# Later turning of the feed-forward products, and more seven-product steps in the down projection

## The chip, the cores and the metric

The kernel runs on one core of one Trainium2 chip. The metric is the device time of one execution in microseconds (us); several executions are summed up by their median. Before the change three runs have a median of 1989.0 us (1987.55 to 1989.62).

## What is computed

An encoder trunk of two layers on 256 tokens of width 2048, all in float32: attention and a feed-forward block, then a gated recurrence and a feed-forward block. The change is in the feed-forward blocks alone:

```python
def swiglu(h, w_gate, w_up, w_down):
    return (jax.nn.silu(h @ w_gate) * (h @ w_up)) @ w_down
...
        x = x + mix
        x = x + swiglu(rms_norm(x, norm_ffn[i]), ffn_w_gate[i], ffn_w_up[i], ffn_w_down[i])
```

The hidden width D_FF is 5632, which is 44 tiles of 128.

## The kernel before

**Products.** Every float32 operand is held as a sum of two parts, `hi` and `lo`, that TensorE takes at full speed, and a product of two blocks is three matmuls (high by high, high by low, low by high; `product`, L342 to L347). The tokens, 128 at a time, are the stationary operand; 512 weight columns stream past them. A weight tile of 128 rows by 1024 elements ("half", `load_half`) comes by DMA on SP's queue (SyncE) into `raw` (5 buffers); ScalarE (ACT) casts it to `hi` (L132) and VectorE (DVE) subtracts to get `lo` (L133), 5 buffers each.

**Pairs.** `project_pair` makes two column blocks (j = 0, 1) for both halves of the tokens (a = 0, 1) at once, in four PSUM accumulators (tag `acc`, 4 buffers in all). A step is two tiles of 128 along the contraction. A plain step is 2 halves and 8 products, 24 matmuls. A seven-product step is Strassen's scheme in Winograd's form on the 2 by 2 blocks (tokens by columns): `seven_forms` makes block sums of the weights, `x_forms` block sums of the left operand, and 7 products, 21 matmuls, do for 8. Such a step loads one half to `raw` as usual, the first half of the next one to `wx` (SP, 256 KB), and that next one whole to `sr` (GpSimd's DMA queue, POOL), whose second part is added onto its first part by an accumulating DMA (L293, L294; 2 buffers, fetched ahead by `fetch_next`). DVE then makes the sums (L307, L311, L312) and three low parts (L313, L315, L316), ACT three casts (L309, L310, L314). `wx`, `wxh` and `wxl` have one buffer each. After the last seven-product step of a pair, `merge` (L380) adds four product sums (tag `pm`) into `fg` and `fu`.

**Feed-forward.** The 44 hidden tiles go in parts of 12, 16 and 16 (PARTS). A part first runs one unit for every 4 hidden tiles: gate and up as a pair of 8 steps, seven-product in steps 2, 4 and 6 (THREE, counted from 0 as 1, 3, 5; the very first unit of a layer has two). At its end `done` applies Silu and the product (L842 to L846), and then the result `fu` is turned so that hidden rows lie on partitions: one block transpose on DVE (L515, `tb`), 16 copies of 32 by 256 on ACT (L523, `tf`), then the split into high and low part (L857 ACT, L858 DVE, `act`). After its 3 or 4 units a part multiplies by its rows of w_down: `down`, two pairs (columns 0 and 1, then 2 and 3). Of the sixteen-tile parts the pairs have 8 steps, seven-product in steps 3 and 6 (TWO); of the twelve-tile part 6 steps, all plain, and the last two steps are taken one column after the other. The second pair of the last part in the first layer has plain steps only, since it feeds the next norm. `done` in `down` adds accumulators to the residual (L575), `middle` the merged sums (L567).

**Order.** TensorE's (PE's) order is that of the program text. The other engines' orders are set by a scheduler at build time, from the text, with the chain of casts (`in_line`) held in order. Each engine runs its list strictly in order.

Of the kernel before, what the change touches and what calls it, by code (L numbers as in the profile page):

```python
# [12 lines left out]
F32 = mybir.dt.float32  # L13
F32R = mybir.dt.float32r
AF = mybir.ActivationFunctionType
ALU = mybir.AluOpType
AX = mybir.AxisListType

P = 128
# [54 lines left out]
def trunk(ctx, tc, w, out):  # L74
# [86 lines left out]
    def down_seven(n, alone):  # L161
        return () if alone or n == SHORT else TWO
# [169 lines left out]

    def project_pair(xs, forms, plan, middle, done):
# [19 lines left out]
        for n, cols in plan:  # L353
            if n in forms:
                s1, s2, s3, s4 = forms[n]
                b11, b21, t3, b22, t1, t2, t4 = seven_forms()
                if n == seven[0]:
                    p1, q6, q5, q7 = (ps_m.tile([P, WIDE], F32, tag="pm", name=nm("pm")) for _ in range(4))
                last = n == seven[-1]
                product(p1, tokens(2 * n, 0), b11, last)  # L360
                product(bank(0, 0), tokens(2 * n + 1, 0), b21)
                product(bank(1, 0), s4, b22)
                product(q7, s3, t3, last)
                product(q5, s1, t1, last)
                product(q6, s2, t2, last)
                product(bank(0, 1), tokens(2 * n + 1, 1), t4)
                if last:
                    middle(p1, q5, q6, q7)
                continue
            end = n == plan[-1][0]  # L370
            for j in cols:
                half()
                hi, lo = (flat(t) for t in newest["tiles"])
                for a in range(2):
                    for k in range(2):
                        product(bank(j, a), tokens(2 * n + k, a), (hi[:, k, :], lo[:, k, :]), end and k == 1)
                if end:
                    done(j, banks[j])
# [132 lines left out]
    def turned(src, both=True, behind=None, whole=False):  # L511
        b = fp[0].tile([P, 2, FOUR, P], F32, tag="tb", name=nm("tb"))
        f = fp[0].tile([P, 8, FOUR, 32], F32, tag="tf", name=nm("tf"))
        if whole:
            dve.transpose(b, src)  # L515
        for a in () if whole else range(2):
            dve.transpose(b[:, a, :, :], src[:, a, :])
# [8 lines left out]
        return f[:].rearrange("p q k t -> p k q t") if whole else [f[:, :, k, :] for k in range(FOUR)]  # L526
# [33 lines left out]
    def down(xs, forms, norm=None, end=False):  # L560
        for c in (0, 2):
# [7 lines left out]
            def done(j, accs):  # L569
                for a in range(2):  # L570
                    n = 2 if end and c + j == NCOL - 1 else 1
                    for i in range(n):
                        sl = slice(i * WIDE // n, (i + 1) * WIDE // n)
# [8 lines left out]
            project_pair(xs, {} if alone else forms, down_plan(len(xs) // 2, alone), middle, done)  # L582
# [247 lines left out]
    def ffn(norm, nxt):  # L830
# [4 lines left out]
        def unit(hid, forms, parts, i):  # L835
# [16 lines left out]
            u = got[1]  # L852
            first = len(hid)
            f = turned(u, False, whole=True)
            h = act_tiles()
            hi, lo = (h[:, :, o : o + S].rearrange("p k (q t) -> p k q t", t=32) for o in (0, S))
            act.copy(hi, f)  # L857
            dve.tensor_tensor(lo, f, hi.bitcast(F32), ALU.subtract)  # L858
            hid.extend(h[:, k, :] for k in range(FOUR))
            for k, n in enumerate(TWO):  # L860
                if parts == KT and first <= 2 * n < len(hid):
                    forms[n] = x_forms(hid[2 * n], hid[2 * n + 1], f"hf{k}")

        line.update(act=None, dve=None)
        for p, n in enumerate(PARTS):
            hid, forms = [], {}
            for i in range(n // FOUR):
                unit(hid, forms, n, sum(PARTS[:p]) // FOUR + i)
# [3 lines left out]
            down(hid, forms, nxt if last else None, last and nxt is None)  # L872
# [221 lines left out]
```

## Time and profile before

| | |
|---|---|
| median of three runs | 1989.0 us |
| profiled execution: its own time | 1986.64 us |
| profiled execution: span, first to last instruction | 1984.7 us |
| DVE busy | 1690.3 us (85%) |
| ACT busy | 1346.5 us (68%) |
| POOL busy | 279.5 us (14%) |
| granted TensorE clock, mean | 1.000 |
| DMA moved, mean rate | 426.98 MB, 215 GB/s |

Busy time is the time in which an engine has at least one instruction under way. On DVE and ACT the spans of neighbours overlap a little, so the distance between two starts in a busy stretch is shorter than the mean duration. Matmuls overlap more, and their pace is read from starts or counts.

### The profile page before, as it was taken

The page shows a single profiled execution, that of the slowest core. Times are in us where ns is not written, and L with a number is a line of the kernel's source. Part 1 is how long each engine was busy: PE and PEld are TensorE (multiplying, and loading weights), DVE is VectorE, ACT ScalarE, POOL GpSimd, SP SyncE. Part 2 cuts the span into 40 slices and gives each one's busy share as a digit, 9 for nine tenths or more (in the row PEclk, how much of TensorE's full clock was granted, in tenths as well). Part 3 has the DMA queues.
Part 4 walks back from the last instruction along what each step waited for, and adds up shares of the span by engine and source line. Part 5 has one row for each costly group of instructions (what it writes and reads, how often), then busy time and mean ns, then how long its engine had stood idle before and what let it go on. Part 6 is the DMA issues. An engine that isn't in the chain of part 4 may idle for free.

```text
span 1984.7 us, 28163 instructions
## 1 busy us (share of the span) xinstructions
PE 1969.9 (99%) x9890; PEld 1676.1 (84%) x9890; DVE 1690.3 (85%) x2355; ACT 1346.5 (68%) x2085; POOL 279.5 (14%) x369
## 2 busy tenths in 40 slices
PE   9999999999999999999999999999999999999999
PEld 8898888888887888888899998888888887888877
DVE  8998788857898888989878977898768998889986
ACT  7666666655777556777799987767646676567763
POOL 2563001000010010001034331001001010011000
PEclk9999999999999999999999999999999999999999
DMA  8444767767677777666655657566757777677773
GB/s 321 158 144 139 226 186 241 241 204 233 212 232 221 249 248 236 205 227 221 207 175 183 191 160 228 190 214 219 249 191 226 230 249 249 204 242 236 232 255 131
DMA packets 131469, 426.98 MB, mean 215 GB/s; under 512 B 14720, under 2 KB 15488, under 8 KB 131200
## 3 DMA queue, kind: packets, MB, share of 16 engines
q1 hardware_dynamic: 108720, 363.81, 53.5%
q0 software_dynamic: 22464, 61.35, 13.1%
q8 instruction: 78, 1.28, 0.3%
q14 instruction: 63, 0.52, 0.1%
q10 hardware_dynamic: 144, 0.02, 0.0%
HBM read 423.03 MB, written 2.10 MB: 214 GB/s over the span
## 4 chain that ended last, share of the span: by engine, by line
PE 72%; DVE 14%; issue 6%; ACT 5%; DMA 2%; POOL 0%; SPq 0%; DVEq 0%; ACTq 0%; POOLq 0%
PE acc L344 40%; PE acc L273 9%; PE pm L344 6%; DVE lo L133 5%; PE acc L251 4%; ACT tf L523 4%; PE acc L391 3%; PE acc L390 3%; PE acc L392 3%; DMA raw<-in_w_gate_dram 1%; PE pm L392 1%; PE pm L391 1%; PE pm L390 1%; DVE lo L313 1%; ACT wxh L314 1%
## 5 line engine op out<-in xcount | busy, mean ns | idle before, releaser
L133 DVE TENSOR_TENSOR lo<-raw,hi 128x1024 fp32r<-128x1024 f32 (+1 forms) x630 | 762.3, 1227 | 164.1 <-ACT hi L132 154.9
L132 ACT CAST hi<-raw 128x1024 fp32r<-128x1024 f32 (+1 forms) x630 | 647.8, 1044 | 346.4 <-PE acc L344 198.5
L344 PE MATMUL acc<-hi,xg 128*128 128x512 f32 x1920 | 613.7, 389 | 1.7 <-DVE fg L842 1.6
L344 PEld LDWEIGHTS acc<-hi,xg 128*128 128x128 f32 x1920 | 360.3, 188 | 77.9 <-DVE fg L842 2.5
L344 PE MATMUL acc<-hi,act 128*128 128x512 f32 x1212 | 378.8, 389 | 0.2 <-DVE fu L845 0.2
L344 PE MATMUL acc<-lo,xg 128*128 128x512 f32 x960 | 373.5, 389 | 0.0
L344 PEld LDWEIGHTS acc<-hi,act 128*128 128x128 f32 x1212 | 227.5, 188 | 47.9 <-issue 0.6
L344 PE MATMUL acc<-lo,act 128*128 128x512 f32 x606 | 235.8, 389 | 0.0
L344 PEld LDWEIGHTS acc<-lo,xg 128*128 128x128 f32 x960 | 180.2, 188 | 37.4
L523 ACT COPY tf<-tb 32x256 f32<-32x256 f32 x448 | 180.7, 403 | 30.7 <-DVE tb L515 24.8
L273 PE MATMUL acc<-hi,act 128*128 128x512 f32 x512 | 160.0, 390 | 0.0
L293 POOL DMA_DIRECT2D sr<-in_w_up_dram x64 | 35.5, 555 | 842.3 <-DVE lo L313 807.7
L391 PE MATMUL acc<-xg,hi 128*128 128x256 f32 x512 | 144.8, 283 | 0.6 <-DVE xg L468 0.6
L390 PE MATMUL acc<-xg,hi 128*128 128x256 f32 x512 | 144.9, 283 | 0.1
L392 PE MATMUL acc<-xg,lo 128*128 128x256 f32 x512 | 144.4, 282 | 0.0
L344 PEld LDWEIGHTS acc<-lo,act 128*128 128x128 f32 x606 | 113.7, 188 | 23.7
L251 PE MATMUL acc<-xg,hi 128*128 128x512 f32 x384 | 126.0, 397 | 0.1
L316 DVE TENSOR_TENSOR wxl<-raw,wxh 128x1024 fp32r<-128x1024 f32 x78 | 95.2, 1220 | 28.6 <-ACT wxh L314 28.6
L314 ACT CAST wxh<-raw 128x1024 fp32r<-128x1024 f32 x78 | 82.0, 1051 | 47.4 <-DVE raw L312 46.5
L273 PEld LDWEIGHTS acc<-hi,act 128*128 128x128 f32 x512 | 96.1, 188 | 19.6
L309 ACT CAST hi<-sr 128x1024 fp32r<-128x1024 f32 x78 | 82.0, 1051 | 44.6 <-PE acc L344 39.4
L273 PE MATMUL acc<-lo,act 128*128 128x512 f32 x256 | 99.6, 389 | 0.0
(246 smaller groups left out, 3289.2 us busy)
## 6 DMA issues: line engine op xcount, KB each, us to landing
raw<-in_w_gate_dram SPq DMA_DIRECT2D x176, 512.0 KB, 5.3
raw<-in_w_down_dram SPq DMA_DIRECT2D x162, 512.0 KB, 4.9
raw<-in_w_up_dram SPq DMA_DIRECT2D x112, 512.0 KB, 5.6
sr<-in_w_up_dram POOLq DMA_DIRECT2D x64, 512.0 KB, 4.7
raw<-in_w_in_dram SPq DMA_DIRECT2D x64, 512.0 KB, 4.4
raw<-in_w_qv_dram SPq DMA_DIRECT2D x40, 512.0 KB, 4.2
raw<-in_w_o_dram SPq DMA_DIRECT2D x32, 512.0 KB, 3.6
wx<-in_w_up_dram SPq DMA_DIRECT2D x64, 256.0 KB, 4.5
```

The lines of the kernel that those rows point to most:

```text
L132: newest["cast"] = in_line("act", act.copy(hi[:, sl, :], raw[:, sl, :]))
L133: in_line("dve", dve.tensor_tensor(lo[:, sl, :], raw[:, sl, :], hi[:, sl, :].bitcast(F32), ALU.subtract))
L251: pe.matmul(o, w, x, start=(k == 0 and not part), stop=(k == total - 1 and not part))
L273: pe.matmul(accs[a], x, wt[:, k, :], start=(k0 + k == 0 and n == 0), stop=(end and k == 1 and n == 2))
L309: in_line("act", act.copy(hi, raw))
L314: in_line("act", act.copy(xh[:, 1:, :], r1))
L316: in_line("dve", dve.tensor_tensor(xl[:, 1:, :], r1, xh[:, 1:, :].bitcast(F32), ALU.subtract))
L344: pe.matmul(acc, a, b, start=id(acc) not in begun, stop=last and i == 2)
L390: pe.matmul(o, hi, x[:, :S], start=start, stop=False)
L391: pe.matmul(o, hi, x[:, S:], start=False, stop=False)
L392: pe.matmul(o, lo, x[:, :S], start=False, stop=stop)
L523: n = turn(o, y)
```

## The change

Three things change. `down_seven` gives the sixteen-tile down pairs seven-product steps 2, 4 and 6 (before: 3 and 6) and the twelve-tile pairs steps 2 and 4 (before: none). `x_forms` is accordingly called for the hidden tiles of the first, second and third unit of a sixteen-tile part and of the first two units of a twelve-tile part. And the turning of a unit's result no longer stands in the text at the unit's end: it is cut into six pieces (transpose, four groups of four copies, split and block sums) that `settle` runs inside the next `project_pair`: three at each seven-product step, one at each half of a plain step that isn't the first, all that are left before a step that takes one column. The copies are held behind the newest cast on ACT. The matrices `tb` and `tf` have the same size as before.

```diff
     def down_seven(n, alone):
-        return () if alone or n == SHORT else TWO
+        return () if alone else THREE[:2] if n == SHORT else THREE
...
+    owed = []
+
+    def settle(n=1):
+        while owed and n:
+            owed.pop(0)()
+            n -= 1
...
-        for n, cols in plan:
+        for i, (n, cols) in enumerate(plan):
             if n in forms:
                 s1, s2, s3, s4 = forms[n]
                 b11, b21, t3, b22, t1, t2, t4 = seven_forms()
+                settle(3)
...
+            if len(cols) == 1:
+                settle(-1)
             end = n == plan[-1][0]
             for j in cols:
                 half()
+                if i:
+                    settle()
...
-            u = got[1]
-            first = len(hid)
-            f = turned(u, False, whole=True)
-            h = act_tiles()
-            hi, lo = (h[:, :, o : o + S].rearrange("p k (q t) -> p k q t", t=32) for o in (0, S))
-            act.copy(hi, f)
-            dve.tensor_tensor(lo, f, hi.bitcast(F32), ALU.subtract)
-            hid.extend(h[:, k, :] for k in range(FOUR))
-            for k, n in enumerate(TWO):
-                if parts == KT and first <= 2 * n < len(hid):
-                    forms[n] = x_forms(hid[2 * n], hid[2 * n + 1], f"hf{k}")
+            def transposes():
+                kept["b"], kept["f"] = (fp[0].tile([P, 2 * FOUR, P], F32, tag=n, name=nm(n), bufs=1) for n in ("tb", "tf"))
+                dve.transpose(kept["b"], got[1])
+
+            def copies(q):
...
+                for i in range(4):
+                    n = act.copy(f[32 * i : 32 * i + 32, q::4, :, :], b[32 * q : 32 * q + 32, :, i, :, :])
+                    follow(n, line["act"])
+
+            def split_tiles():
...
+                act.copy(hi, f)
+                dve.tensor_tensor(lo, f, hi.bitcast(F32), ALU.subtract)
+                hid.extend(h[:, k, :] for k in range(FOUR))
+                for k, n in enumerate(THREE):
+                    if n in down_seven(parts // 2, False) and first <= 2 * n < len(hid):
+                        forms[n] = x_forms(hid[2 * n], hid[2 * n + 1], f"hf{k}")
+
+            owed.extend([transposes, *(partial(copies, q) for q in range(4)), split_tiles])
```

In the orders below a name stands for a buffer's use (`act_2701` is one unit's split hidden tiles), and line numbers of the changed kernel are larger by some lines: L842/L852 and L845/L855 take accumulators into `fg` and `fu`, L846/L856 make the hidden product, L515/L869 transpose, L523/L875 copy, L857/L882 and L858/L883 split, L575/L585 release accumulators, L383 to L386 / L395 to L398 merge, L567/L577 add the merged sums.

**First place: DVE where the first twelve-tile down pair of the second layer begins.** Before:

```order
L845 TENSOR_TENSOR fu_2686_14230<-acc_2641_14011,fu_2686_14230 128x512
L846 SCALAR_TENSOR_TENSOR fu_2686_14230<-fu_2686_14230,nr_2483_13212,fg_2685_14229 128x512 x2
L133 TENSOR_TENSOR lo_2720_14416<-raw_2718_14414,hi_2719_14415 128x1024
L515 STREAM_TRANSPOSE tb_2699_14316<-fu_2686_14230 128x1024
L133 TENSOR_TENSOR lo_2723_14434<-raw_2721_14432,hi_2722_14433 128x1024
L133 TENSOR_TENSOR lo_2726_14452<-raw_2724_14450,hi_2725_14451 128x1024
L133 TENSOR_TENSOR lo_2729_14470<-raw_2727_14468,hi_2728_14469 128x1024
L858 TENSOR_TENSOR act_2701_14335<-tf_2700_14317,act_2701_14335 128x4x256
```

Now, the same stretch up to the transpose and the next load:

```order
L855 TENSOR_TENSOR fu_2731_14383<-acc_2681_14132,fu_2731_14383 128x512
L856 SCALAR_TENSOR_TENSOR fu_2731_14383<-fu_2731_14383,nr_2524_13345,fg_2730_14382 128x512
L312 TENSOR_TENSOR raw_2754_14509<-raw_2754_14509 128x512
L313 TENSOR_TENSOR lo_2761_14521<-sr_2711_14264,hi_2760_14520 128x1024
L315 TENSOR_TENSOR wxl_2759_14517<-wx_2757_14515,wxh_2758_14516 128x512
L856 SCALAR_TENSOR_TENSOR fu_2731_14383<-fu_2731_14383,nr_2524_13345,fg_2730_14382 128x512
L316 TENSOR_TENSOR wxl_2759_14517<-raw_2754_14509,wxh_2758_14516 128x1024
L133 TENSOR_TENSOR lo_2771_14571<-raw_2769_14569,hi_2770_14570 128x1024
L869 STREAM_TRANSPOSE tb_2763_14533<-fu_2731_14383 128x1024
L133 TENSOR_TENSOR lo_2774_14593<-raw_2772_14591,hi_2773_14592 128x1024
```

and a little later, up to the low half of the split:

```order
L313 TENSOR_TENSOR lo_2782_14625<-sr_2729_14358,hi_2781_14624 128x1024
L315 TENSOR_TENSOR wxl_2780_14621<-wx_2778_14619,wxh_2779_14620 128x512
L316 TENSOR_TENSOR wxl_2780_14621<-raw_2775_14613,wxh_2779_14620 128x1024
L133 TENSOR_TENSOR lo_2789_14674<-raw_2787_14672,hi_2788_14673 128x1024
L133 TENSOR_TENSOR lo_2792_14692<-raw_2790_14690,hi_2791_14691 128x1024
L883 TENSOR_TENSOR act_2784_14637<-tf_2764_14534,act_2784_14637 128x4x256
```

The transpose now stands behind the whole set of block sums of step 2, and the low half of the split behind those of step 4 and two more loads, where only plain loads stood.

**Second place: ACT where a sixteen-tile down pair of the second layer begins.** Before:

```order
L309 CAST hi_3088_16333<-sr_3033_16032 128x1024
L310 CAST wxh_3086_16329<-wx_3085_16328 128x512
L523 COPY tf_3064_16225<-tb_3063_16224 32x2x128 x16
L314 CAST wxh_3086_16329<-raw_3082_16322 128x1024
L132 CAST hi_3096_16372<-raw_3095_16371 128x1024
L132 CAST hi_3099_16390<-raw_3098_16389 128x1024
L132 CAST hi_3102_16408<-raw_3101_16407 128x1024
L132 CAST hi_3105_16426<-raw_3104_16425 128x1024
L857 CAST act_3065_16243<-tf_3064_16225 128x4x256
L132 CAST hi_3108_16444<-raw_3107_16443 128x1024
```

Now:

```order
L309 CAST hi_3150_16504<-sr_3101_16248 128x1024
L310 CAST wxh_3148_16500<-wx_3147_16499 128x512
L603 ACTIVATE fg_3120_16366<-fg_3120_16366,nr_2524_13345 128x512
L314 CAST wxh_3148_16500<-raw_3144_16493 128x1024
L132 CAST hi_3160_16554<-raw_3159_16553 128x1024
L132 CAST hi_3163_16576<-raw_3162_16575 128x1024
L132 CAST hi_3166_16598<-raw_3165_16597 128x1024
L309 CAST hi_3171_16608<-sr_3119_16342 128x1024
L875 COPY tf_3154_16518<-tb_3153_16517 32x2x128 x16
L310 CAST wxh_3169_16604<-wx_3168_16603 128x512
L314 CAST wxh_3169_16604<-raw_3165_16597 128x1024
```

The sixteen copies still stand together on ACT. Before, they stood between the first (L310) and the second (L314) cast of the block sums of the pair's first seven-product step, step 3; now they stand ahead of both of these casts of the second one, step 4, and step 2 has its casts ahead of them.

**Third place: DVE at the end of the first column of that twelve-tile pair.** The two accumulators of column 0 are `acc_2705` and `acc_2706` before, `acc_2747` and `acc_2748` now; the second pair takes over the four buffers in the order in which the first took them. Before:

```order
L133 TENSOR_TENSOR lo_2749_14584<-raw_2747_14582,hi_2748_14583 128x1024
L575 TENSOR_TENSOR x_tok_75<-x_tok_75,acc_2705_14344 128x512
L575 TENSOR_TENSOR x_tok_75<-x_tok_75,acc_2706_14351 128x512
L133 TENSOR_TENSOR lo_2754_14604<-raw_2752_14602,hi_2753_14603 128x1024
L133 TENSOR_TENSOR lo_2757_14622<-raw_2755_14620,hi_2756_14621 128x1024
```

Now:

```order
L585 TENSOR_TENSOR x_tok_75<-x_tok_75,acc_2747_14475 128x512
L397 TENSOR_TENSOR fg_2785_14661<-pm_2768_14547,fg_2785_14661 128x512
L398 TENSOR_TENSOR fu_2786_14662<-fu_2786_14662,pm_2768_14547 128x512
L577 TENSOR_TENSOR x_tok_75<-x_tok_75,fu_2786_14662 128x512
L133 TENSOR_TENSOR lo_2811_14790<-raw_2809_14788,hi_2810_14789 128x1024
L307 TENSOR_TENSOR wx_2812_14794<-wx_2812_14794,raw_2809_14788 128x512
L577 TENSOR_TENSOR x_tok_75<-x_tok_75,fg_2785_14661 128x512
L577 TENSOR_TENSOR x_tok_75<-x_tok_75,fu_2786_14662 128x512
L585 TENSOR_TENSOR x_tok_75<-x_tok_75,acc_2752_14495 128x512
L311 TENSOR_TENSOR raw_2809_14788<-sr_2762_14530,raw_2809_14788 128x512
L585 TENSOR_TENSOR x_tok_75<-x_tok_75,acc_2748_14482 128x512
```

Two neighbours have come apart: nine instructions now stand between the release of column 0's first accumulator and that of its second. The end of the first pair of the last part in the first layer looks alike.

34 lines of the change are left out of this document (20 added, 14 removed).

## The prediction

> **What bounds the kernel now.** I read the page's head, then windows over the stages of the second layer's feed-forward, then TensorE's waits, then the timelines of the places where it waits. First the head, an undisturbed window, and four stages: the first twelve-tile down pair, the first and the third unit of a sixteen-tile part, and that part's first down pair. The columns are the stretch, its length, then PE, PE's weight loads, DVE, ACT and POOL (busy time and instructions), the granted clock, DMA share and rate.
>
> ```profile
> span 1984.7 us, 28163 instructions
> PE 1969.9 (99%) x9890; PEld 1676.1 (84%) x9890; DVE 1690.3 (85%) x2355; ACT 1346.5 (68%) x2085; POOL 279.5 (14%) x369
> 1430.00:1590.00 160.00, 160.00 (x707) 132.48 (x707) 127.35 (x144) 94.97 (x120) 11.86 (x17) 1.00 0.70 222
> 1410.80:1443.50 32.70, 32.70 (x146) 27.09 (x145) 21.56 (x22) 19.88 (x30) 0.00 (x0) 1.00 0.66 212
> 1517.60:1559.10 41.50, 41.50 (x185) 34.37 (x184) 36.93 (x43) 29.08 (x42) 4.23 (x6) 1.00 0.76 241
> 1600.70:1642.30 41.60, 41.60 (x184) 34.10 (x183) 39.36 (x50) 30.05 (x43) 4.24 (x6) 1.00 0.75 231
> 1642.30:1685.50 43.20, 41.81 (x183) 34.06 (x182) 37.07 (x43) 27.89 (x39) 2.82 (x4) 1.00 0.71 233
> ```
>
> TensorE sets the time: 706 intervals in 160 us are 0.2266 us per matmul, and 160 us pass without a gap, at a clock of 1.00. So a matmul that goes away in a feed-forward stage takes 0.2266 us with it, as long as the engines that feed it keep up. DVE comes next: it has 2.2 us to spare in the third unit (41.60 less 39.36), 11 us in the twelve-tile pair. Now the only waits of any weight in those stages, and one of the four places in detail, TensorE's starts first, then ACT, then DVE:
>
> ```profile
> PE pm L344 <- DVE wxl L316: 3.0, 4, 0.8
> PE pm L344 <- ACT wxh L314: 2.3, 4, 0.7
> ...
> 1656.33 0.39 PE L344 MATMUL pm<-wxh,hf 128*128 128x512 f32 x1
> 1657.35 0.50 PE L344 MATMUL pm<-wxh,hf 128*128 128x512 f32 x1 [0.63 <-ACT wxh L314]
> 1658.61 0.50 PE L344 MATMUL pm<-wxl,hf 128*128 128x512 f32 x1 [0.76 <-DVE wxl L316]
> 1658.95 0.40 PE L344 MATMUL pm<-wxh,hf 128*128 128x512 f32 x1
> ...
> 1646.51 0.62 ACT L310 CAST wxh<-wx 128x512 fp32r<-128x512 f32 x1 [0.21 <-DVE wx L307]
> 1649.59 6.63 ACT L523 COPY tf<-tb 32x256 f32<-32x256 f32 x16 [2.46 <-DVE tb L515]
> 1656.25 1.04 ACT L314 CAST wxh<-raw 128x1024 fp32r<-128x1024 f32 x1
> 1657.20 3.89 ACT L132 CAST hi<-raw 128x1024 fp32r<-128x1024 f32 x4
> ...
> 1648.32 1.24 DVE L515 STREAM_TRANSPOSE tb<-fu 128x1024 f32<-128x1024 f32 x1
> 1657.33 1.23 DVE L316 TENSOR_TENSOR wxl<-raw,wxh 128x1024 fp32r<-128x1024 f32 x1 [5.46 <-ACT wxh L314]
> ```
>
> The reader is to see a queue: the 16 copies that turn the last unit's result take ACT 6.63 us, the cast L314 stands behind them, DVE's L316 behind that, and TensorE behind both. Three intervals (1656.33 to 1658.95) take 2.62 us instead of 0.68: 1.94 us lost, where the waits view counts 1.39 (0.63 and 0.76). There are four such places, one at the start of each sixteen-tile down. Scaled from 1.39 to 1.94, their 5.3 us in the waits view (3.0 and 2.3) are 7.4 us.
>
> **The change part by part.**
>
> *Fewer matmuls.* A seven-product step has 21 matmuls for 24. The first layer gains two in each of two twelve-tile pairs and one in each of three sixteen-tile pairs (the fourth stays plain), the second layer two in two and one in four: 7 and 8. 15 steps by 3 matmuls by 0.2266 us are 10.2 us less.
>
> The Trainium skill, "TensorE: Matmul & The Clock Gate", section "Wait — 56ns, not 53.3ns?", gives 215.7 ns between starts for 512 columns on a warm array; the trace has 226.6 here, and the measurement decides. By the page it would be an estimated 9.7 us.
>
> *More work on DVE, ACT and DMA.* Their prices come from the page's groups and a busy stretch of DVE:
>
> ```profile
> L133 DVE TENSOR_TENSOR lo<-raw,hi 128x1024 fp32r<-128x1024 f32 (+1 forms) x630 | 762.3, 1227 | 164.1 <-ACT hi L132 154.9
> L316 DVE TENSOR_TENSOR wxl<-raw,wxh 128x1024 fp32r<-128x1024 f32 x78 | 95.2, 1220 | 28.6 <-ACT wxh L314 28.6
> ...
> 1601.57 0.68 DVE L311 TENSOR_TENSOR raw<-sr,raw 128x512 f32<-128x512 f32 x1
> 1602.17 0.68 DVE L845 TENSOR_TENSOR fu<-acc,fu 128x512 f32<-128x512 f32 x1
> 1606.43 1.22 DVE L316 TENSOR_TENSOR wxl<-raw,wxh 128x1024 fp32r<-128x1024 f32 x1
> 1607.57 1.22 DVE L133 TENSOR_TENSOR lo<-raw,hi 128x1024 fp32r<-128x1024 f32 x1
> ```
>
> From start to start a 128x512 operation takes 0.60 us and a 128x1024 one 1.14. A plain step costs DVE two L133, 2.28 us; a seven-product step three of 1.14 (L133, L313, L316) and four of 0.60 (L307, L311, L312, L315), 5.82: 3.54 more, 53 us over 15 steps. TensorE needs 24 x 0.2266 = 5.44 us for a plain step and 4.76 for the other. The block sums of the hidden tiles are made 16 times, not 8; the third unit, which has one set, shows 2.4 us more DVE than the first, which has none, so 8 x 2.4 = 19 us. All this lies beside TensorE if each stage keeps room. The twelve-tile pair: 21.56 + 2 x 3.54 = 28.6 us of DVE in 32.70 - 2 x 0.68 = 31.3. The sixteen-tile pair: 37.07 + 3.54 = 40.6 in 43.2 - 1.9 - 0.7 = 40.6, level, but a unit with three such steps runs today at 39.36 of 41.60 without a gap, the next pair has one set of turning fewer, and five buffers carry loads over. I take nothing, and DVE's overrun as a rival. ACT gains 1.7 us a step (two 1.04 and one 0.62 for one 1.04), at 19.88 of 32.70. DMA gains 0.5 MB a step, 7.5 MB of 427; the units have the same density and run at shares of 0.75 and 0.76. Thirty more POOL DMAs are fetched ahead through two buffers as in the units. Without that cover the 53 us would lie open, more than five times the gain.
>
> *The four stalls.* After the change step 2 of a sixteen-tile down has its casts ahead of the copies, and the copies stand before L310 of step 4 (second place in the orders). Are they done then? The pair begins at 1642.3 and the transpose ends 7.3 us later (1649.56). In front of it now stand L312, L313 and L315 as well, 2.3 us: 9.6. Copies 6.63, cast 0.62, L315 0.68: 17.5. TensorE wants that at 5.44 + 4.76 + 5.44 and 12 matmuls of step 4 (2.7), at 18.4. There are 0.9 us in hand, so the four stalls go, 7.4 us; at worst they come back whole.
>
> *A new wait in the twelve-tile pair.* Its step 5 uses the last unit's tiles. The rows before:
>
> ```profile
> 1410.78 0.39 PE L344 MATMUL acc<-hi,act 128*128 128x512 f32 x1
> 1411.06 1.22 DVE L133 TENSOR_TENSOR lo<-raw,hi 128x1024 fp32r<-128x1024 f32 x1 [0.61 <-ACT hi L132]
> 1415.86 1.24 DVE L515 STREAM_TRANSPOSE tb<-fu 128x1024 f32<-128x1024 f32 x1
> 1427.15 1.22 DVE L858 TENSOR_TENSOR act<-tf,act 128x1024 fp32r<-128x1024 f32 x1
> 1437.69 1.28 DVE L575 TENSOR_TENSOR x_tok<-x_tok,acc 128x512 f32<-128x512 f32 x2
> 1417.13 6.64 ACT L523 COPY tf<-tb 32x256 f32<-32x256 f32 x16 [2.33 <-DVE tb L515]
> ```
>
> The pair begins at 1410.8, the transpose ends at +6.3 and the low half at +17.6; step 5 begins at 4 x 5.44 = +21.8, so 4 us were spare. Now step 5 begins at 2 x 5.44 + 2 x 4.76 = +20.4. Ahead of the transpose stand all block sums of step 2 (the first place): L307, L311, L312, L315 at 0.60 and L313, L316 at 1.14, 4.7 us, so +11.0 if all of it comes on top. But L307 and L311 stand ahead of the instructions that wait for the unit's last products and so fit into DVE's waiting (1.2 us), as does perhaps the 0.61 in the row: +9.2 to +11.0. The copies: 6.64 more. Then L310 and L314 (0.62 and 1.04) and, on DVE, L316 and two L133 (3 x 1.14) and L883 (1.22): 6.3 more. The low half is there at +22.1 to +23.9, and TensorE waits 1.7 to 3.5 us. I take 2.0, near the lower end, since DVE and ACT were held by full buffers before this place and will use the room. Two layers: 4.0 us. Below this, nothing if the sums of step 2 are done before the pair begins.
>
> *A new wait at the change of pairs.* The second pair's second accumulator waits for the release of column 0's second one. Today the two releases run in 1.28 us, at 1437.69. Now nine instructions stand between them (third place), eight of 0.60 and one of 1.14, 5.9 us; with the first release 0.60 and the second 0.68 it is free 7.2 us after the first begins, which is up to 0.7 late behind a load. TensorE comes there 5.44 us (column 1) and six matmuls (1.4), 6.8 us after column 0 ended: a wait of 0.4 to 1.1. I take 1.0. It occurs in the two twelve-tile downs and at the last part of the first layer: 3.0 us. Nothing if the scheduler's list runs early, 1.9 each if a load more is in the way.
>
> *Sum.* -10.2 - 7.4 + 4.0 + 3.0 = -10.6 us, on the profiled execution's own 1986.64 (span 1984.7 and 1.9 around it): 1976.0. The median of the runs shown is 2.4 above that execution, 1989.0, so I forecast 1978.4.
>
> **The rivals.**
>
> *DVE becomes the bound* (slower). Place: the sixteen-tile pairs and the units behind them, 7 pairs with one step more and 16 units, with the 4 twelve-tile pairs 27 stages. For it: the level sum above, 39.36 of 41.60, and DVE's 5.46 us wait on ACT, which would count as DVE time. Against it: three such units run one after another without a gap. The gain of 10.6 is used up at 0.4 us overrun per stage; at 0.7 us, 18.9 come back: 1997.
>
> *The copies hold the next casts instead* (no change). The 16 copies are still one block ahead of L310 and L314. If the 0.9 us in hand is not there, four stalls of 1.9 stay, and the twelve-tile wait is 3.5: -10.2 + 7.0 + 3.0 = -0.2, 1988.8. For it: the same block costs 1.94 today. Against: it now has 10 us more.
>
> *No new waits.* If DVE runs far enough ahead, both new waits vanish: -17.6, 1971.4.
>
> *The second tiles come late from POOL* (slower). Each of 15 steps needs one more fetch through GpSimd's queue beside a fuller DVE.
>
> ```profile
> L294 POOL DMA_DIRECT2D sr<-in_w_up_dram x64 | 55.3, 863 | 269.8 <-DMA sr<-in_w_up_dram 261.5 <-issue 8.3
> L294 POOL DMA_DIRECT2D sr<-in_w_down_dram x14 | 12.1, 861 | 58.0 <-DMA sr<-in_w_down_dram 52.8 <-issue 5.2
> ```
>
> Against it: the issue takes 863 ns in most of the units' fetches and 861 in those for the downs, though DVE's load differs. If every one of the 30 issues waited out one L133 (1.14 us) and none of it were hidden, 34 us: 2013.
>
> The Trainium skill, "SBUF — State Buffer", section "SBUF: two separate sides", says that GpSimd cannot write a DMA's descriptors while a VectorE instruction holds their shared port; this rule is what would make that rival true. The two equal rows don't show it.
>
> **How the numbers follow.** The forecast has 0.74, the copies 0.10, no new waits 0.07, DVE 0.07, POOL 0.02. A measurement of this kernel tells 0.2% (4 us) from no change. The forecast's own range is -15 to -6 (either new wait at its ends), 1974 to 1983, and faster; so is the case without waits. The copies' case is within 0.2% but for a part that ends faster: same 0.09. Slower is 0.07 and 0.02, 0.09; faster the rest, 0.82. The range runs from 1972, near the case without waits, to 1987, which takes in most of the copies' case and leaves out the two slower ones.
>
> **What would show it.** In the changed profile: 45 matmuls fewer in the feed-forward lines; 93 instances of L313 for 78; no waits of `pm` on L314 and L316 at the start of the sixteen-tile downs; instead about 2 us on L883 in each twelve-tile down, and about 1 us on a release (L585) at the start of its second pair; units still without gaps. Wrong would be: gaps in the third or fourth unit of a part or before a `wxl` (DVE at 99% there), or `sr` landing after L309 is due.

## The result, and the profile after

The changed kernel takes 1978.1 us (median of six, 1976.92 to 1979.95) beside 1989.3 for the kernel before in runs on the same chip (six, 1987.55 to 1991.80): a ratio of 0.9943 with a 95% interval of 0.9932 to 0.9953. Its profiled execution takes 1977.2 us, 9.4 less than the 1986.64 of before; by the spans, from first to last instruction, the gain is 9.3 (1984.7 to 1975.4). First the head of the changed kernel's page:

```profile
span 1975.4 us, 28389 instructions
PE 1960.1 (99%) x9845; PEld 1666.7 (84%) x9845; DVE 1774.7 (90%) x2518; ACT 1370.9 (69%) x2127; POOL 301.5 (15%) x399
```

TensorE has 45 matmuls fewer (9890 to 9845), DVE 84 us more work, ACT 24. Now the windows of one twelve-tile and one sixteen-tile down of the second layer, from first matmul to first matmul of what follows, before the change:

```profile
1410.80:1476.06 65.26, 65.26 (x289) 54.04 (x288) 39.99 (x40) 33.89 (x44) 0.00 (x0) 1.00 0.61 196
1642.27:1728.59 86.32, 84.93 (x373) 69.74 (x372) 72.15 (x84) 48.72 (x62) 5.64 (x8) 1.00 0.70 226
```

and the same two stages after it, with a unit of the sixteen-tile part between them:

```profile
1407.18:1472.55 65.37, 63.75 (x277) 51.46 (x276) 61.83 (x75) 39.81 (x53) 5.66 (x8) 1.00 0.71 232
1555.70:1597.20 41.50, 41.50 (x184) 34.35 (x184) 39.25 (x50) 29.96 (x43) 4.24 (x6) 1.00 0.72 235
1638.72:1722.16 83.44, 83.26 (x368) 68.62 (x366) 79.20 (x94) 51.11 (x65) 8.50 (x12) 1.00 0.75 246
```

The twelve-tile down has 12 matmuls fewer, worth 2.7 us at 0.2266, and is no shorter: PE, busy without a break before, now misses 1.6 us of the stretch. The sixteen-tile down is 2.9 us shorter. The unit (184 matmuls in 41.50 us) keeps its old pace. So the gain lies in the sixteen-tile downs, in three of the four: by windows of this kind 2.9 us in each layer's first and 3.2 in the second layer's last, while the first layer's last down is no shorter (87.71 before, 87.87 now). TensorE's waits in the changed kernel say why:

```profile
PE acc L351 <- DVE x_tok L585: 2.3, 4, 1.3
PE acc L351 <- DVE act L883: 2.2, 2, 1.1
...
PE acc L351 <- DVE lo L133: 1.0, 1, 1.0
...
PE acc L351 <- ACT act L882: 0.3, 2, 0.2
PE pm L351 <- DVE wxl L316: 0.2, 1, 0.2
```

The waits of `pm` on the casts, 5.3 us before, are down to 0.2. In their place stand waits on the split hidden tiles (L882, L883) and on the releases (L585), which the profile before did not have. The timeline of the sixteen-tile down that the prediction looked at, now (ACT, then DVE, then TensorE):

```profile
1643.33 1.05 ACT L314 CAST wxh<-raw 128x1024 fp32r<-128x1024 f32 x1 [3.00 <-DVE raw L312]
1644.28 2.95 ACT L132 CAST hi<-raw 128x1024 fp32r<-128x1024 f32 x3
1647.13 1.05 ACT L309 CAST hi<-sr 128x1024 fp32r<-128x1024 f32 x1
1648.08 6.64 ACT L875 COPY tf<-tb 32x256 f32<-32x256 f32 x16
1654.74 0.62 ACT L310 CAST wxh<-wx 128x512 fp32r<-128x512 f32 x1
...
1644.95 1.24 DVE L869 STREAM_TRANSPOSE tb<-fu 128x1024 f32<-128x1024 f32 x1
1655.39 0.69 DVE L315 TENSOR_TENSOR wxl<-wx,wxh 128x512 fp32r<-128x512 f32 x1 [1.50 <-ACT wxh L310]
...
1657.31 0.39 PE L351 MATMUL pm<-wxl,hf 128*128 128x512 f32 x1
```

The sixteen copies still take 6.64 us in one piece. But the casts of step 2 (L314) and of step 3 (three L132) are done before they begin, and TensorE lives on those two steps while ACT copies. L315 of step 4 ends at 1656.08, 17.4 us after the pair began at 1638.72, and TensorE takes it at 1657.31 without a wait.

The twelve-tile down (DVE's transpose and low half, then TensorE's starts) and the change of pairs behind it (three releases, then TensorE) look like this:

```profile
1416.00 1.23 DVE L869 STREAM_TRANSPOSE tb<-fu 128x1024 f32<-128x1024 f32 x1
1428.95 1.22 DVE L883 TENSOR_TENSOR act<-tf,act 128x1024 fp32r<-128x1024 f32 x1
...
1427.85 0.40 PE L351 MATMUL acc<-wxh,act 128*128 128x512 f32 x1
1428.40 0.50 PE L351 MATMUL acc<-hi,act 128*128 128x512 f32 x1 [0.16 <-ACT act L882]
1428.74 0.40 PE L351 MATMUL acc<-lo,act 128*128 128x512 f32 x1
1430.22 0.73 PE L351 MATMUL acc<-hi,act 128*128 128x512 f32 x2 [1.08 <-DVE act L883]
...
1436.42 0.68 DVE L585 TENSOR_TENSOR x_tok<-x_tok,acc 128x512 f32<-128x512 f32 x1
1441.76 0.68 DVE L585 TENSOR_TENSOR x_tok<-x_tok,acc 128x512 f32<-128x512 f32 x1
...
1442.96 0.68 DVE L585 TENSOR_TENSOR x_tok<-x_tok,acc 128x512 f32<-128x512 f32 x1
...
1441.91 0.39 PE L351 MATMUL acc<-hi,act 128*128 128x512 f32 x1
1442.49 0.50 PE L351 MATMUL acc<-hi,act 128*128 128x512 f32 x1 [0.20 <-DVE x_tok L585]
```

The low half is ready at 1430.17, 23.0 us after the pair's begin, and TensorE starts on it 0.05 us later. The bracket behind a matmul undercounts: the interval that holds a wait is longer than 0.2266 us by 0.32 (1427.85 to 1428.40) and 1.25 (1428.74 to 1430.22), and the one after a wait takes 0.34 instead of 0.2266 (1428.40 to 1428.74), 0.11 more. Below, "by starts" means that waits are counted so. At the change of pairs the wait ends with the second release in DVE's list (1441.76 to 1442.44); the third (1442.96), that of column 0's second accumulator, has not begun by then.

### The profile page after: what moved, and what is told of

Read it like the earlier page. It is cut to its first block, busy times and chain, and to the rows that moved or that the text cites. A ratio compares the mean times of both kernels' runs of the same rounds, so it can differ in the third digit from the quotient of the medians.

```text
span 1975.4 us, 28389 instructions
## 1 busy us (share of the span) xinstructions
PE 1960.1 (99%) x9845; PEld 1666.7 (84%) x9845; DVE 1774.7 (90%) x2518; ACT 1370.9 (69%) x2127; POOL 301.5 (15%) x399
## 4 chain that ended last, share of the span: by engine, by line
PE 71%; DVE 13%; issue 6%; ACT 6%; DMA 3%; POOL 0%; SPq 0%; DVEq 0%; ACTq 0%; POOLq 0%
PE acc L351 37%; PE acc L273 9%; PE pm L351 8%; PE acc L251 4%; DVE lo L133 4%; ACT tf L875 3%; PE acc L403 3%; PE acc L402 3%; PE acc L404 3%; DMA raw<-in_w_down_dram 1%; PE pm L404 1%; PE pm L402 1%; PE pm L403 1%; ACT hi L132 1%; DVE lo L313 1%
## 5 line engine op out<-in xcount | busy, mean ns | idle before, releaser
L133 DVE TENSOR_TENSOR lo<-raw,hi 128x1024 fp32r<-128x1024 f32 (+1 forms) x615 | 741.5, 1225 | 92.0 <-ACT hi L132 83.5
L132 ACT CAST hi<-raw 128x1024 fp32r<-128x1024 f32 (+1 forms) x615 | 628.8, 1043 | 247.7 <-PE acc L351 89.9
L351 PE MATMUL acc<-hi,act 128*128 128x512 f32 x1002 | 320.7, 390 | 4.9 <-DVE x_tok L585 2.3
L351 PEld LDWEIGHTS acc<-hi,act 128*128 128x128 f32 x1002 | 187.9, 188 | 47.6 <-DVE x_tok L585 4.5
L351 PE MATMUL acc<-lo,act 128*128 128x512 f32 x501 | 195.1, 389 | 1.0 <-DVE lo L133 1.0
L314 ACT CAST wxh<-raw 128x1024 fp32r<-128x1024 f32 x93 | 97.7, 1051 | 96.1 <-DVE raw L312 95.9
L273 PE MATMUL acc<-hi,act 128*128 128x512 f32 x512 | 160.0, 390 | 0.0
L875 ACT COPY tf<-tb 32x256 f32<-32x256 f32 x352 | 142.1, 404 | 14.0 <-DVE tb L869 10.1
L293 POOL DMA_DIRECT2D sr<-in_w_up_dram x64 | 35.6, 557 | 688.0 <-DVE lo L313 572.0
L310 ACT CAST wxh<-wx 128x512 fp32r<-128x512 f32 x93 | 57.7, 621 | 106.0 <-DVE wx L307 75.0
L309 ACT CAST hi<-sr 128x1024 fp32r<-128x1024 f32 x93 | 97.7, 1051 | 41.5 <-PE acc L351 33.1
L316 DVE TENSOR_TENSOR wxl<-raw,wxh 128x1024 fp32r<-128x1024 f32 x93 | 113.3, 1218 | 7.7 <-ACT wxh L314 7.5
L313 DVE TENSOR_TENSOR lo<-sr,hi 128x1024 fp32r<-128x1024 f32 x93 | 113.2, 1217 | 0.0
L273 PEld LDWEIGHTS acc<-hi,act 128*128 128x128 f32 x512 | 96.1, 188 | 19.6
```

Of the source, the lines that this page charges most:

```text
L132: newest["cast"] = in_line("act", act.copy(hi[:, sl, :], raw[:, sl, :]))
L133: in_line("dve", dve.tensor_tensor(lo[:, sl, :], raw[:, sl, :], hi[:, sl, :].bitcast(F32), ALU.subtract))
L273: pe.matmul(accs[a], x, wt[:, k, :], start=(k0 + k == 0 and n == 0), stop=(end and k == 1 and n == 2))
L309: in_line("act", act.copy(hi, raw))
L313: in_line("dve", dve.tensor_tensor(lo, raw, hi[:].bitcast(F32), ALU.subtract))
L316: in_line("dve", dve.tensor_tensor(xl[:, 1:, :], r1, xh[:, 1:, :].bitcast(F32), ALU.subtract))
```

## The experiments

Ratios are to the kernel before, on the same chip; e1 to e4 share one chip (before: 1989.5), e5 to e8 one (1991.6), e9 and e10 one (1989.9). The changed kernel was timed beside another before (1989.3), so a difference from it is read from the ratios or from the spans of the profiled executions; a plain difference of medians across these groups can be off by the 2.3 us that lie between the befores. Expected sizes were missed in several: e2 is 1.6 us slower than the slower end of its theory A, and e3 to e7 are 0.5 to 3.0 us faster than the faster end of theirs. Line numbers move by some lines where an edit adds lines: the low half's L883 is L858 in e1, L892 in e5, L894 in e9 and e10; the release L585 is L575 in e1, L592 in e4, L586 in e8.

**e1. The steps without the later turning.** The kernel before with the new steps and nothing else.

```diff
     def down_seven(n, alone):
-        return () if alone or n == SHORT else TWO
+        return () if alone else THREE[:2] if n == SHORT else THREE
...
-            for k, n in enumerate(TWO):
-                if parts == KT and first <= 2 * n < len(hid):
+            for k, n in enumerate(THREE):
+                if n in down_seven(parts // 2, False) and first <= 2 * n < len(hid):
```

> The kernel before with the new seven-product steps alone; the turning stays in the text at the unit's end. Theory A (the places of the steps decide: with steps 2 and 4 in front, the copies fall behind the first casts whatever the text says, since DVE and ACT run in the scheduler's order, and that order comes out the same as the changed kernel's): same time as the changed kernel, 1978 within 2 us; no wait of pm on L314 or L316, about 2.2 us in two waits on the split's low half (now at its old line) in the twelve-tile downs. Theory B (putting the turning later took the four stalls away): the stalls stay, 7.4 us more than the changed kernel, about 1985.5, with the waits view at 5 us or more on pm for L314 and L316.

1976.6 us (1974.27 to 1980.98), ratio 0.9937 (0.9924 to 0.9950), span 1975.4: the changed kernel's own. Its waits are the changed kernel's too (2.2 us on the releases, 2.2 on the low half). Half of the change does nothing: at build time the scheduler puts the work of ACT and DVE in the same order with either text, and the two lists read alike row for row but for the buffers' numbers.

**e2. The later turning alone.** The changed kernel with the old steps (3 and 6, none in the twelve-tile downs).

```diff
-        return () if alone else THREE[:2] if n == SHORT else THREE
+        return () if alone or n == SHORT else TWO
...
-                for k, n in enumerate(THREE):
+                for k, n in enumerate(TWO):
```

> The changed kernel with the old seven-product steps (3 and 6 of the sixteen-tile downs, none in the twelve-tile ones). 45 matmuls come back, 10.2 us. Theory A (the steps' places decide): the copies' 6.6 us block still meets the casts near step 3, only at another load; part of the four stalls stays, 1 to 1.7 us each, so 2 to 4 us less than before: 1985 to 1987. Theory B (later turning removes the stalls): 7.4 us less than before, 1982, with no wait of TensorE at the start of the sixteen-tile downs.

1988.6 us (1985.88 to 1991.81), ratio 0.9995 (0.9987 to 1.0004): no gain, where theory A had expected 2 to 4 us. Here the order does change. ACT at the start of the same sixteen-tile down, and TensorE's waits:

```profile
1654.44 1.65 ACT L875 COPY tf<-tb 32x256 f32<-32x256 f32 x4 [2.46 <-DVE tb L869]
1656.11 1.06 ACT L314 CAST wxh<-raw 128x1024 fp32r<-128x1024 f32 x1
1657.19 4.97 ACT L875 COPY tf<-tb 32x256 f32<-32x256 f32 x12
```

```profile
PE acc L351 <- DVE lo L133: 3.0, 4, 0.8
...
PE acc L351 <- ACT hi L132: 2.0, 4, 0.7
```

Four copies now stand ahead of the cast L314 and twelve behind it. The four stalls on that cast are gone, and four on the next load's cast and low part (5.0 us together, 5.3 before) have come instead. The block was cut, and the stall moved one load on. What removes the stalls in the changed kernel is that the seven-product steps stand at 2 and 4, so that the casts of step 2 and of the plain step 3 are ahead of the block.

**e3. No seven-product steps in the twelve-tile downs.**

```diff
-        return () if alone else THREE[:2] if n == SHORT else THREE
+        return () if alone or n == SHORT else THREE
```

> The changed kernel without seven-product steps in the twelve-tile downs. The windows of the changed kernel show the two twelve-tile downs at 65.4 us each against 65.8 and 65.3 before, so their 24 saved matmuls (5.4 us) were eaten by waits. Theory A (the waits come from those steps): the waits on L883 and on the release in the twelve-tile downs go, 24 matmuls come back, and the time stays at 1977 to 1978. Theory B (the waits come from the turning and stay): 5.4 us slower than the changed kernel, 1983.5.

1976.5 us (1975.39 to 1978.17), ratio 0.9935 (0.9921 to 0.9948), span 1973.8. With 24 matmuls more than the changed kernel it is no slower: the eight new steps, 5.4 us of matmuls, pay for their own waits and no more. No wait on the low half is left; the releases wait 0.8 us, once.

**e4. One step in the twelve-tile downs, releases first.** Only step 2 is seven-product there, and an accumulator pair is released before the merged sums are added to the residual (not in the last down, where the sums stay ahead).

```diff
-        return () if alone else THREE[:2] if n == SHORT else THREE
+        return () if alone else THREE[:1] if n == SHORT else THREE
...
-                g, u = merge(*banks)
-                for j, t in enumerate((g, u)):
-                    for a in range(2):
-                        y = x_tok[:, a, c + j, :]
-                        dve.tensor_tensor(y, y, t[:, a, :], ALU.add)
+                sums[:] = merge(*banks)
+                if end:
+                    add_sums(0)
+                    add_sums(1)
+            sums = []
+            def add_sums(j):
+                for a in range(2) if sums else ():
+                    y = x_tok[:, a, c + j, :]
+                    dve.tensor_tensor(y, y, sums[j][:, a, :], ALU.add)
...
+                if not end:
+                    add_sums(j)
```

> The changed kernel with step 2 alone as seven-product step in the twelve-tile downs, and with the merged sums added to the residual after the accumulators' release and not before (not so in the kernel's last down). Theory A (the low half is late by the block sums of step 4, and the release is late by the instructions between the two): step 5 begins 0.7 us later and one set of block sums (4.7 us) less stands before the low half, so no wait there and none on the release: 12 matmuls back (2.7 us), waits of 2.2 and 2.3 us and their unseen part (1.5 us) gone: 3 to 5 us less than the changed kernel, 1973.5 to 1975. Theory B (DVE's total is the limit in that down, and waits only move): the saved wait turns up elsewhere, 1978 to 1981.

1972.3 us (1970.43 to 1974.31), ratio 0.9913 (0.9899 to 0.9926), span 1970.3. The low half's wait is gone, and a release is waited for once (1.1 us), in the last down, which kept its order. The interval overlaps that of e5, which keeps both steps, so the gain can be the releases' alone.

**e5. Releases first, both steps kept.** The second part of e4's edit alone.

> The changed kernel, both seven-product steps kept in the twelve-tile downs, with the merged sums added to the residual after the accumulators' release (not so in the kernel's last down). Theory A (the release is late by the instructions between the two releases): the four waits on the release (2.3 us in the waits view) and the one on a load behind it (1.0) go, those on the low half (2.2, with the unseen part about 3) stay: 3 to 4 us less than the changed kernel, 1974 to 1975. Theory B (DVE's total is the limit): the adds only come later and the time stays, 1978.

1972.2 us (1971.72 to 1973.00), ratio 0.9902 (0.9887 to 0.9917), span 1971.2. Of the two kinds of wait the one on the low half is left in full, and no release is waited for:

```profile
PE acc L351 <- DVE act L892: 2.2, 2, 1.1
```

The new wait at the change of pairs was thus a matter of the order of the merged sums and the releases. It cost more than its 2.3 us in the view (3.8 by starts, below): the span falls by 4.2.

**e6. The kernel before with one copy** in place of the sixteen. The rearrangement across partitions is left out.

```diff
-        for q in range(4):
+        if whole:
+            act.copy(f[:].rearrange("p q k t -> p (q k t)"), b[:].rearrange("p a i t -> p (a i t)"))
+        for q in () if whole else range(4):
```

> The kernel before with the turning's 16 copies replaced by one copy of the same 128x1024 elements (about 1.05 us on ACT for 6.6); the rearrangement between partitions is left out, so the hidden tiles hold other values. Theory A (the copies on ACT hold up the cast L314): no waits of pm on L314 and L316, 7 to 9 us less than before, 1980.5 to 1982.5. Theory B (the first seven-product step of a down is late for another reason, its loads or its block sums on DVE): the waits stay, 1988 to 1989.5.

1977.5 us (1976.94 to 1978.27), ratio 0.9929 (0.9913 to 0.9946), span 1975.0, 9.7 below before's 1984.7. No wait on L314 or L316 is left. The sixteen copies were the whole cause of the four stalls (7.5 us by starts, below). Of the other 2 us, 0.5 is a wait on `fu` at the start of the first layer's twelve-tile down (TensorE's starts at 396.20 and 396.83 before), which is gone too; the rest is spread in small pieces. The six downs together take 473.2 us for 481.5. By the medians the gain is larger, 14.1 us; the last section comes back to that.

**e7. The changed kernel with one copy**, the same part left out.

```diff
-                for i in range(4):
-                    n = act.copy(f[32 * i : 32 * i + 32, q::4, :, :], b[32 * q : 32 * q + 32, :, i, :, :])
-                    follow(n, line["act"])
+                if q == 0:
+                    follow(act.copy(kept["f"], kept["b"]), line["act"])
```

> The changed kernel with the same replacement, the rearrangement left out. Theory A (the low half comes late by the block sums and the 6.6 us of copies): it comes 5.6 us sooner, so the waits on the low half (2.2 us in view, about 3 in all) go, and with DVE sooner free those on the release too: 5 to 8 us less than the changed kernel, 1970 to 1973. Theory B (the low half is late by DVE's own queue): DVE has nothing less to do, so at least half of the waits stay, 1975 to 1978.

1967.0 us (1966.91 to 1967.33), ratio 0.9876 (0.9861 to 0.9891), span 1965.1, 10.3 below the changed kernel's. The waits on the low half and on the releases are both gone: one copy takes ACT 1.05 us for 6.64. The six downs take 463.0 us for the changed kernel's 472.4, and no wait of TensorE is left in them. So the copies cost 9.4 us in these downs, 8.3 in those of the kernel before: the change did not make them cheaper, it moved their cost to other waits. Without them it is worth its matmuls alone, 10.2 us in the downs (473.2 to 463.0).

**e8. More DVE work in the downs.** The changed kernel with L316 done twice in each of the 29 seven-product steps of the downs, 29 x 1.14 = 33 us of DVE.

```diff
-        in_line("dve", dve.tensor_tensor(xl[:, 1:, :], r1, xh[:, 1:, :].bitcast(F32), ALU.subtract))
+        for _ in range(1 + more):
+            in_line("dve", dve.tensor_tensor(xl[:, 1:, :], r1, xh[:, 1:, :].bitcast(F32), ALU.subtract))
```

> The changed kernel with L316 issued twice in each seven-product step of the downs (29 steps, 1.14 us each, 33 us of DVE work that computes the same values again). Theory A (DVE has only about 1 to 3 us to spare in a down pair, and the added 2.3 to 3.4 us per pair use that up): about half of the 33 us shows, 10 to 22 us more than the changed kernel, 1988 to 2000. Theory B (DVE's work lies beside TensorE with room to spare, as the 53 us of the change did): less than 5 us more, 1983 at most.

1998.2 us (1992.14 to 2000.23), ratio 1.0030 (1.0018 to 1.0042): 20 us above the changed kernel. Its waits:

```profile
PE acc L352 <- DVE x_tok L586: 11.7, 8, 3.4
PE pm L352 <- DVE wxl L317: 7.5, 11, 1.0
```

By the spans it is 22 us (1997.5 for 1975.4). Not all of that is DVE: the granted clock stood at 0.50 for 13.65 us in the downs of this execution (last section), which makes up to 6.8 us. The other 15 are a little under half of the added 33. So DVE's work in the downs is hidden today with some 0.6 us a step to spare, an estimate (33 less 15 us over 29 steps).

**e9 and e10. Four and eight of the sixteen copies on GpSimd**, on top of e5 (for e10 the condition is `i > 1`).

```diff
-                    n = act.copy(f[32 * i : 32 * i + 32, q::4, :, :], b[32 * q : 32 * q + 32, :, i, :, :])
-                    follow(n, line["act"])
+                    put = pool.tensor_copy if i == 3 else act.copy
+                    n = put(f[32 * i : 32 * i + 32, q::4, :, :], b[32 * q : 32 * q + 32, :, i, :, :])
+                    if put == act.copy:
+                        follow(n, line["act"])
```

> The changed kernel with the releases first (1972.2, span 1971.2) and four of the sixteen copies of each turning on POOL. Theory A (the block of copies on ACT alone sets the low half's time in the twelve-tile downs, POOL is free): ACT's block falls from 6.64 to 12 x 0.415 = 5.0 us, the wait on the low half in each twelve-tile down from 1.2 us to nothing or 0.3, the time to 1969 to 1970.5. Theory B (POOL's list is strict, and the copies stand there between two fetches of sr, the second part of which waits for the first to land; DVE's work beside it also counts): the four copies come later than ACT's twelve, the wait on the low half stays or grows above 2 us each, and the next fetch is late: 1973 to 1980.

> The same with eight of the sixteen copies on POOL. Theory A: ACT's block is 3.3 us; the wait on the low half is gone if POOL's eight take less than 6.6 us: 1968.5 to 1970. Theory B: POOL's eight copies are slower than ACT's sixteen were and hold the fetches behind them: waits on the low half of 2 us and more, waits on sr: 1975 to 1990.

Four: 1970.2 us (1969.13 to 1971.54), ratio 0.9900 (0.9885 to 0.9914), span 1967.4. Eight: 1991.9 us (1986.48 to 1999.34), ratio 1.0014 (1.0002 to 1.0026). With four the time is near theory A's, but not for its reason. ACT in the second layer's twelve-tile down, DVE's low half there, and the wait in the view:

```profile
1412.96 4.98 ACT L885 COPY tf<-tb 32x256 f32<-32x256 f32 x12 [0.38 <-DVE tb L878]
1417.96 1.05 ACT L314 CAST wxh<-raw 128x1024 fp32r<-128x1024 f32 x1
...
1422.46 1.22 DVE L894 TENSOR_TENSOR act<-tf,act 128x1024 fp32r<-128x1024 f32 x1
```

```profile
PE acc L351 <- DVE act L894: 1.9, 2, 1.1
```

The block on ACT is 5.0 us, as expected, but the scheduler put it between L310 and L314 of step 4 (the changed kernel has it ahead of both), so the low half still waits behind that cast. Against e5 the intervals overlap; the two are not told apart. With eight, the time is just above theory B's, mostly by a way that it did not name: next to 3.0 us on the low half stand waits on `fu` and `fg`, with which a unit frees its accumulators, 12.9 us; on `sr` there is none.

```profile
PE acc L351 <- DVE fu L864: 7.5, 9, 1.2
PE acc L351 <- DVE fg L861: 5.4, 6, 1.8
```

One piece of that is in the timelines of POOL and DVE in a unit:

```profile
1618.70 8.28 POOL L885 COPY tf<-tb 32x256 f32<-32x256 f32 x8
...
1621.83 1.41 DVE L313 TENSOR_TENSOR lo<-sr,hi 128x1024 fp32r<-128x1024 f32 x1
```

Beside the copies DVE's 128x1024 operations last 1.41 us for 1.22 (last section), and POOL's next fetch (L293) waits for the eight. How much of the 12.9 us each of the two makes was not tried.

## Why the prediction was right

It forecast 1978.4 us and the time is 1978.1. That the two meet to 0.3 us is in part luck: the sum put the profiled execution at 1976.0, and it took 1977.2; the 2.4 us by which the median lay above the profiled execution were carried over, and they are 0.9 now. The sum's terms, one by one, waits counted by starts:

- **45 matmuls fewer, 10.2 us.** As said: x9845, at the old pace in the units.
- **Four stalls, 7.4 us.** Before they were 7.5 us in all (1.94 at the place that was shown), and they are gone. L315 of step 4 was put at 17.5 us behind the pair's begin and came at 17.4, but not by the way that was worked out. The transpose ended at 7.5 us (1646.19), not 9.6; the copies began only at 9.4, since ACT had five casts (L314, three L132, L309) to do from 1643.33 to 1648.08, which the working did not count. The margin, put at 0.9 us, was 1.2 (1656.08 to 1657.31). What it left open is which half of the change does it, and e1 and e2 answer: the places of the steps, not the later turning.
- **The wait on the low half, 4.0 us for two layers.** In the second layer 0.32 and 1.25, an earlier 0.34 on L316, and 0.11 behind each of the three: 2.2; in the first 1.8. Together 4.0. The waits just ahead (L316, L882) count with it: without them TensorE would have come sooner and stood that much longer at the low half. The transpose ended 10.05 us and the low half 23.0 us behind the pair's begin, inside the bounds of 9.2 to 11.0 and 22.1 to 23.9. e3 and e4 show the wait gone with step 4.
- **The wait at the change of pairs, 3.0 us at three places.** 0.5, 1.0 and 1.5 (the last at the first layer's last part): 3.0. The size is right and one step of it is not: the buffer that the second pair waits for is freed by the second release in DVE's list, column 1's first, and not by column 0's second (the buffers are not handed on in the order in which the first pair took them), so in the second layer it is free 6.0 us behind the start of the first release (1436.42 to 1442.44), where 7.2 was worked out. In its place the first release is later than the 0.7 us that were allowed: TensorE was due at 1442.14 (1441.91 and 0.23), 6.8 us after column 0 ended, so column 0 ended at 1435.3 and its first release began 1.1 us later. The two errors nearly cancel, which is luck.
- **What the sum left out:** the same release late at two sixteen-tile changes of pairs (0.3 and 0.5) and a low part L133 late in the first layer's last pair (1.0 in the view, 1.2 by starts): 2.0 us. The terms with these make -8.7, and the wait on `fu` that is gone (0.5, see e6) -9.2; the spans differ by 9.3. In the first layer's last down the late release (1.5) and the late L133 (1.2) use up what its three matmuls fewer and its stall (0.7 and 2.0) gave.
- **DVE's 53 and 19 us at nothing.** The busy time grew by 84 us, not 72. Right in the units, which keep their pace, and thinner than it looks in the downs: the 2.0 us left out are waits on DVE, and 33 us more there cost some 15 beside the clock (e8). The rival "DVE becomes the bound" had the right place, the pairs, but not the amount. The rival of late second tiles did not occur: no `sr` shows in TensorE's waits.
- **"The copies hold the next casts instead"** did not come in the changed kernel at those places; it is what e2 does. In sum the copies cost as much as before (e6, e7), which the forecast has in its -7.4 and +7.0 but does not say.

## What to carry to other kernels

Ask of a long block in a strict queue what the waiting engine has to live on while it runs, and move its customers rather than the block: having two steps' casts done ahead of the block removed four stalls that cutting it in pieces only shifted. Then ask where the block's cost went: here it came back as other waits. After a step has become cheaper, look at what frees the buffers for the next one: releasing the accumulators before adding sums that nobody waits for gave 4 us by the spans (e5), beside 9 for the whole change. And a text that is written in another order may be the same program once a scheduler has put it in order.

## What the runs showed of the hardware

The granted clock falls to 0.50 behind short gaps of TensorE, and their length alone does not decide it. TensorE's starts in e8, at the change of pairs of the first layer's twelve-tile down and of its last down, and windows after them (the granted clock is the third figure from the end; the count of matmuls, behind the second figure, is of those under way):

```profile
427.73 0.39 PE L352 MATMUL acc<-hi,act 128*128 128x512 f32 x1
431.56 0.50 PE L352 MATMUL acc<-hi,act 128*128 128x512 f32 x1 [3.45 <-DVE x_tok L586]
...
930.05 0.50 PE L352 MATMUL acc<-hi,act 128*128 128x512 f32 x1 [1.93 <-DVE x_tok L586]
```

```profile
433.00:435.00 2.00, 1.19 (x3) 0.50 (x3) 2.00 (x5) 2.00 (x3) 0.55 (x1) 0.50 0.14 25
435.00:437.00 2.00, 2.00 (x6) 1.54 (x6) 1.97 (x3) 0.09 (x1) 0.00 (x0) 0.50 0.95 250
...
441.00:443.00 2.00, 2.00 (x10) 1.67 (x9) 1.97 (x3) 1.05 (x1) 0.00 (x0) 1.00 1.05 301
...
931.00:933.00 2.00, 2.00 (x6) 1.57 (x5) 1.97 (x5) 0.72 (x2) 0.00 (x0) 0.50 1.00 331
```

Behind the gap of 3.45 us the clock is at 0.50 for 6.8 us (432.42 to 439.24), behind that of 1.93 us for 3.4 (930.76 to 934.18), and so behind a third, of 2.83 us (1456.42 to 1459.83). At 0.50 TensorE begins a matmul every 0.43 us (436.44 to 436.87) instead of 0.23, so such a gap can cost about twice its length, and more than the waits view says. The starts in e10 after a gap of 1.53 us and after one of 1.84, and a window behind each:

```profile
418.93 0.99 PE L351 MATMUL acc<-hi,act 128*128 128x512 f32 x2 [1.53 <-DVE act L894]
...
1652.20 0.50 PE L351 MATMUL acc<-hi,act 128*128 128x512 f32 x1 [1.84 <-DVE fg L861]
...
420.00:422.00 2.00, 2.00 (x6) 1.51 (x6) 2.00 (x4) 0.00 (x0) 0.00 (x0) 0.50 1.03 395
1652.00:1654.00 2.00, 1.80 (x8) 1.50 (x9) 2.00 (x5) 0.93 (x3) 0.00 (x0) 1.00 0.02 10
```

The shorter gap is followed by 0.50, the longer one is not. In e2 two gaps of 0.73 and 0.77 us, which end at 897.14 and 898.40, are enough (0.52 from 901 to 903). The Trainium skill, "TensorE: Matmul & The Clock Gate", section "What's actually happening", has the array at half rate after an idle window of about 3.4 us. The 0.50 agrees; but the clock also fell after gaps of 1.93 and 1.53 us, where by that figure it would not have. In the profiled execution of the changed kernel, whose longest such gap is 1.28 us, the mean clock is 1.000.

This bears on the medians. On the chip of e5 to e8 the executions of the kernel before have a mean clock from 1.000 (1987.28 us at the fastest) to 0.997 (1994.22), those of e5, e6 and e7 all have 1.000. It fits that the four stalls, two gaps of up to 0.76 us each time, sometimes cost the clock, and that this is the rest of e6's 14.1 us; it is not shown, for no such execution of the kernel before was profiled.

DVE and GpSimd slow each other down, and do so by turns. Two of GpSimd's copies in e10:

```profile
646.42 0.40 POOL L885 COPY tf<-tb 32x256 f32<-32x256 f32 x1
1622.21 1.29 POOL L885 COPY tf<-tb 32x256 f32<-32x256 f32 x1
```

The first runs while DVE does nothing. The second begins 0.38 us behind the start of DVE's L313 (1621.83, above) and ends at 1623.50, 0.26 us after that operation, so it takes 0.9 us longer. L313 in turn lasts 1.41 us for 1.22. The Trainium skill, "SBUF — State Buffer", section "SBUF: two separate sides", says that of two such operations on the shared port one waits for the other's whole length. The trace agrees for the copy; DVE's operation, which began 0.33 us before the copy ahead of it ended (1622.16), is 0.19 us longer and no more.
